# Latent attention whose keys and queries come transposed out of their products, with one product for all rotary parts and another order of the first layer's loads and splits

## Chip, core and metric

The kernel runs on one core of a Trainium2 chip. The metric is the device time of one execution in microseconds. The core has TensorE for matrix products (PE; PEld is its load of the stationary operand), VectorE (DVE), ScalarE (ACT), GpSimd (POOL), and SyncE (SP), which here only issues the transfers. Products land in PSUM, eight banks of 128 partitions by 512 words; everything else is held in SBUF with 128 partitions.

## What is computed

A decoder of four layers on 256 tokens of width 1024. Layers 0 and 3 mix tokens by multi-head latent attention, layer 1 by a convolution, layer 2 by a gated recurrence; every layer then has a SwiGLU feed-forward and an embedding that is gated by the residual stream. The change touches the attention of layers 0 and 3 and the start of layer 0. Cut to that:

```python
def _mla(u, positions, w_in, q_norm_g, w_uq, kv_norm_g, w_ukv, w_out):
    c = u @ w_in                                  # 1024 -> 384 + 256 + 32
    c_q, c_kv, k_r = jnp.split(c, [384, 640], axis=-1)
    q = (_rmsnorm(c_q, q_norm_g) @ w_uq).reshape(B, S, 16, 64 + 32)
    kv = (_rmsnorm(c_kv, kv_norm_g) @ w_ukv).reshape(B, S, 16, 64 + 64)
    q_nope, q_rope = jnp.split(q, [64], axis=-1)
    k_nope, v = jnp.split(kv, [64], axis=-1)
    q_rope, k_rope = _rope(q_rope, cos, sin), _rope(k_r, cos, sin)
    q = concat([q_nope, q_rope]); k = concat([k_nope, k_rope for every head])
    o = _causal_attention(q, k, v, 96 ** -0.5)    # 16 heads, softmax over earlier tokens
    return o.reshape(B, S, 1024) @ w_out
```

## The kernel before

All large products are made in three partial products of rounded halves. An operand x is split into hi (x rounded to the matrix format) and lo (the rest): for activations in `split`, hi on ACT (L237) and lo on DVE (L238), for weights in `granule`, hi on ACT (L180, or L185 with a gain folded in) and lo on DVE (L181, L186). `mm` then issues hi·hi, hi·lo and lo·hi (all L207). Weights come in granules of 128 rows by 1024 words by one transfer each (L176 on SP) into four `raw` buffers, are split into nine `whi` and eight `wlo` buffers, and are used once. A later granule's load thus waits until a raw buffer has been split, and its split until an earlier granule has been used. `self.fence` names an instruction on ACT and one on DVE behind which the next splits are put into the queues; `issue_after` does that for a block.

The program is written as one sequence; a list scheduler interleaves it into the queues of the engines by program order and readiness, and each engine then runs its queue in order.

**The start (`run`).** The gains and the first 128 tokens are loaded, `mla_setup` loads the positions, makes the causal mask and computes the rotation angles in some thirty small DVE operations, then the first input weight is loaded and split, `Norm.do(0)` takes squares of the tokens on ACT (L73) and transposes them on TensorE (L250) into the split operand xT, then the same for the other 128 tokens, then the other seven input weights.

**The head of an attention layer (`mla`).** For each of two halves of 128 tokens the input projection lands in two PSUM banks, is copied (`cg`), squared for the second norm, transposed and split into the operand cT (640 rows by 256 tokens). In layer 0 `rope_tables` takes the sine (L535). A chain of small DVE operations (`rsqrt`) makes the scales `sc` of the second norm, and the rotary key `krot` is rotated.

**The heads.** `heads(gi)` makes the queries, keys and values of four heads. For each half of the tokens it multiplies cT (stationary) with the query weights (4 x 96 = 384 columns) and with the key and value weights (512 columns). Tokens lie on partitions, so that ACT applies the scale per token when it evicts the queries (L619) and the values (L625), and DVE that of the keys (L622). POOL copies the rotated key into each head (L623), DVE rotates the queries' last 32 columns (L549 to L552), and TensorE transposes each head's queries and keys, 128 x 96 to 96 x 128 (L631), eight transposes for each half of the tokens, which ACT (L635) and DVE (L637) evict into qT and kT.

**Attention.** `attend(gi)` takes a group in two steps of two heads: scores of both token blocks into two banks (L645 to L650), maxima on DVE (L652 to L654), exponentials with row sums on ACT (L659), scaling by the reciprocal on DVE and ACT (L666, L668), transposes (L672 to L678), evictions (L675, L679) and the weighted sums (L682, L684). `heads(gi)` is issued before `attend(gi - 1)`.

**The end of the layer.** Behind the last group's heads, the output weights (eight granules) are loaded and split, in layer 0 after the layer's embedding weights (`embed_weights`), and the embedding's 24 products (`embed`) are issued after the last `attend`. The first six k-tiles of the output projection of the first tokens can run before the last group is done (`linear`, with `early`).

## Time and profile before

| | us |
|---|---|
| median of 3 runs | 1402.48 |
| lowest and highest of them | 1398.79, 1409.24 |
| the profiled execution | 1401.64 |
| its span, from first to last instruction | 1399.9 |
| layer 0: input projection done, first scores, last weighted sum, feed-forward | 31.2, 50.5, 116.6, 135.6 |
| layer 3: the same | 1082, 1102.4, 1164.4, 1175.4 |
| granted TensorE clock, mean | 0.993 |

The times of the stages are read from the timeline. A group's row gives the source line, engine and operation, what it writes and reads, the shapes, the count, and behind the bar the busy time and the mean ns of one, then the idle time of the engine before it and what ended that. A row of the timeline gives start, duration, and the same names. A matmul's duration there runs until its last result has landed, and so overlaps the next one's.

### The profile page before, as it was taken

To read this page: it belongs to the slowest core of one execution; us is meant where nothing else is said; L and a number is where in the kernel's file an instruction comes from. 1 tells how busy PE (TensorE), PEld (TensorE's weight loads), DVE (VectorE), ACT (ScalarE), POOL (GpSimd) and SP (SyncE) were. 2 spreads that over 40 slices of the span, in tenths; PEclk is the share of its full clock that TensorE was granted. 3 is DMA by queue.
4 is the path that set the end of the run, shared out by engine and by line. 5 is a ranking of instruction groups with operands and counts; after the bars stand their busy time and mean duration, and the time that the engine had idled before them with its cause. 6 is when DMAs were issued, how large, how long until landed. Compare 5 with 4: busy or idle time off the path is not lost.

```text
span 1399.9 us, 20414 instructions
## 1 busy us (share of the span) xinstructions
PE 1340.7 (96%) x7153; PEld 1094.1 (78%) x7153; DVE 920.0 (66%) x1995; ACT 789.0 (56%) x1493; POOL 15.6 (1%) x51
## 2 busy tenths in 40 slices
PE   7889999999898999999999999999999999999997
PEld 6757878887886788888788887878878767788885
DVE  6774555548786855556887768555567776555556
ACT  6684545546625754455675546555556776554543
POOL 0000000000000000000000000000000000000000
PEclk9999999999999999999999999999999999999998
DMA  7242655555674666554474435655553433666632
GB/s 217 94 140 87 210 181 181 181 180 167 187 226 153 187 196 190 181 181 142 132 223 125 140 91 166 195 181 181 181 171 111 136 121 108 207 192 190 187 126 76
DMA packets 174023, 228.15 MB, mean 163 GB/s; under 512 B 11712, under 2 KB 138848, under 8 KB 173920
## 3 DMA queue, kind: packets, MB, share of 16 engines
q1 hardware_dynamic: 173920, 226.85, 52.1%
q8 instruction: 56, 0.92, 0.3%
q14 instruction: 47, 0.39, 0.1%
HBM read 222.27 MB, written 1.05 MB: 160 GB/s over the span
## 4 chain that ended last, share of the span: by engine, by line
PE 76%; DVE 8%; DMA 7%; ACT 6%; issue 3%; SPq 0%; DVEq 0%; ACTq 0%
PE mm L207 41%; PE acc L207 26%; PE tr L250 3%; DVE wlo L186 3%; DMA raw<-in_ffn_w_down_dram 2%; DMA raw<-in_ple_w_gate_dram 1%; PE acc L1013 1%; ACT whi L180 1%; ACT whi L185 1%; DMA raw<-in_mla_w_out_dram 1%; ACT p L659 1%; DVE wlo L181 1%; PE acc L649 1%; DMA raw<-in_ffn_w_gu_dram 1%; DMA raw<-in_conv_w_pw_dram 1%
## 5 line engine op out<-in xcount | busy, mean ns | idle before, releaser
L207 PE MATMUL mm<-whi,xT 128*128 128x512 f32 x1632 | 546.8, 398 | 1.2 <-ACT xT L237 0.9
L185 ACT ACTIVATE whi<-raw,gT 128x512 fp32r<-128x512 f32 (+3 forms) x604 | 387.0, 701 | 133.4 <-PE acc L207 59.7
L186 DVE SCALAR_TENSOR_TENSOR wlo<-raw,gT,whi 128x512 fp32r<-128x512 f32 (+3 forms) x604 | 410.1, 728 | 52.0 <-PE acc L207 33.1
L207 PEld LDWEIGHTS mm<-whi,xT 128*128 128x128 f32 x1632 | 305.6, 188 | 63.5 <-ACT xT L237 1.4
L207 PE MATMUL mm<-wlo,xT 128*128 128x512 f32 x816 | 320.6, 393 | 1.1 <-DVE wlo L181 1.1
L207 PE MATMUL acc<-whi,aT 128*128 128x512 f32 x704 | 233.1, 392 | 1.7 <-DVE aT L238 1.7
L181 DVE TENSOR_TENSOR wlo<-raw,whi 128x1024 fp32r<-128x1024 f32 x120 | 146.7, 1224 | 75.3 <-ACT whi L180 75.0
L180 ACT ACTIVATE whi<-raw 128x1024 fp32r<-128x1024 f32 x120 | 126.0, 1059 | 95.3 <-DMA raw<-in_ffn_w_down_dram 58.2
L207 PEld LDWEIGHTS mm<-wlo,xT 128*128 128x128 f32 x816 | 153.6, 188 | 30.6 <-DVE wlo L181 1.4
L207 PE MATMUL acc<-whi,xT 128*128 128x512 f32 (+2 forms) x544 | 167.1, 382 | 6.2 <-ACT xT L237 6.2
L207 PEld LDWEIGHTS acc<-whi,aT 128*128 128x128 f32 x704 | 131.5, 188 | 35.3 <-DVE aT L238 4.1
L207 PE MATMUL acc<-wlo,aT 128*128 128x512 f32 x352 | 138.7, 394 | 0.0
L364 DVE SCALAR_TENSOR_TENSOR ga<-mm,rs_y,sg 128x256 f32<-128x256 f32 x88 | 42.4, 481 | 139.9 <-ACT sg L362 139.9
L207 PEld LDWEIGHTS acc<-whi,xT 128*128 128x128 f32 x544 | 100.5, 190 | 22.4 <-ACT xT L237 7.0
L362 ACT ACTIVATE sg<-mm,rs_y 128x256 f32<-128x256 f32 x88 | 41.0, 466 | 134.8 <-PE mm L207 134.7
L207 PE MATMUL acc<-wlo,xT 128*128 128x512 f32 (+2 forms) x272 | 101.9, 375 | 0.0
L207 PEld LDWEIGHTS acc<-wlo,aT 128*128 128x128 f32 x352 | 66.2, 188 | 13.0
L238 DVE TENSOR_TENSOR aT<-tr,aT 128x256 fp32r<-128x256 f32 x88 | 37.0, 421 | 55.3 <-ACT aT L237 55.3
L207 PEld LDWEIGHTS acc<-wlo,xT 128*128 128x128 f32 x272 | 51.7, 190 | 7.6
L207 PE MATMUL mm<-whi,cT 128*128 128x384 f32 (+1 forms) x160 | 51.4, 381 | 5.7 <-ACT q L619 4.7
L73 ACT ACTIVATE junk<-h 128x512 bf16<-128x512 f32 x48 | 30.0, 625 | 45.8 <-DVE h L339 25.0
L237 ACT ACTIVATE aT<-tr 128x256 fp32r<-128x256 f32 x88 | 32.7, 371 | 28.1 <-PE tr L250 28.0
(250 smaller groups left out, 1455.4 us busy)
## 6 DMA issues: line engine op xcount, KB each, us to landing
raw<-in_ffn_w_gu_dram SPq DMA_DIRECT2D x352, 256.0 KB, 4.4
raw<-in_ffn_w_down_dram SPq DMA_DIRECT2D x88, 512.0 KB, 4.3
raw<-in_ple_w_gate_dram SPq DMA_DIRECT2D x32, 512.0 KB, 4.7
raw<-in_hgrn_w_in_dram SPq DMA_DIRECT2D x64, 256.0 KB, 3.8
raw<-in_mla_w_out_dram SPq DMA_DIRECT2D x16, 512.0 KB, 4.4
raw<-in_conv_w_pw_dram SPq DMA_DIRECT2D x32, 256.0 KB, 4.8
raw<-in_mla_w_in_dram SPq DMA_DIRECT2D x16, 336.0 KB, 3.8
raw<-in_mla_w_uq_dram SPq DMA_DIRECT2D x12, 384.0 KB, 3.8
```

Of the source, the lines that this page charges most:

```text
L73: square = nc.scalar.activation(T.tmp("junk", [P, 512], 1, BF16), h[:, s], AF.Square, accum_out=ss[:, c : c + 1])
L180: nc.scalar.activation(hi[:, :used], raw[:, :used], AF.Copy)
L181: nc.vector.tensor_tensor(out=lo[:, :used], in0=raw[:, :used], in1=hi[:, :used].bitcast(F32), op=ALU.subtract)
L185: nc.scalar.activation(hi[:, s], raw[:, s], AF.Copy, scale=g[k])
L186: nc.vector.scalar_tensor_tensor(out=lo[:, s], in0=raw[:, s], scalar=g[k], in1=hi[:, s].bitcast(F32), op0=ALU.mult, op1=ALU.subtract)
L207: ins = self.nc.tensor.matmul(*args, **kw)
L237: a = self.nc.scalar.activation(hi, src, AF.Copy)
L238: v = self.nc.vector.tensor_tensor(out=lo, in0=src, in1=hi.bitcast(F32), op=ALU.subtract)
L250: nc.tensor.transpose(pt[:, (i - k0) * P : (i - k0 + 1) * P], src[:, i * P : (i + 1) * P], self.ident)
L362: nc.scalar.activation(sg, ps[:, :256], AF.Silu, scale=r)
L364: nc.vector.scalar_tensor_tensor(out=ga, in0=ps[:, 256:], scalar=r, in1=sg, op0=ALU.mult, op1=ALU.mult)
L649: nc.tensor.matmul(s1[:, hh], qT[:HD, h, P:], kT[:HD, h], start=True, stop=False)
```

## The change

**Products.** The weights are laid out anew on the host: all heads' plain query columns, then all rotary query columns; all keys, then all values. Queries and keys are now made with the weights as the stationary operand and cT, all 256 tokens wide, as the moving one, so that they come out with head channels on partitions and tokens along the columns. One product holds two heads (2 x 64 channels); `queries` evicts the lower 64 partitions on ACT and the upper 64 on DVE, `keys` both on DVE. The scale of a key is no longer one per partition: it is spread over columns by a product of ones with a diagonal matrix (`kscale`) and multiplied in at the eviction. The queries stay unscaled; their scale goes into the softmax, per token (`scl`, `nscl`). Values are made for eight heads at once.

**Rotary parts.** The rotary query columns of all 16 heads come out of one product per half of the tokens, are rotated at once (`rope` with 512 columns) and transposed four heads at a time (`rotary`). The rotated key is repeated four times, transposed, and copied by POOL into its 32 rows of each head's keys. A head's 96 channels lie among 128 rows, and the rows that belong to other heads are zero in the keys (`memset`), so the scores contract over 128 rows.

**The first layer.** The tokens are loaded first, then the gains, then the weights; the tokens' transposes come before the squares of the norm, which are put behind the last split of the input weights; the masks and the angles come after all input weights; the embedding's weights are loaded and split before attention, and its products run right after the input projection.

```diff
-            for t in range(NT):
-                ss, r = css[t], norm.r[t]
...
             if i == 0:
+                self.embed(0)
                 self.rope_tables()
...
+            ws = weights(0)
+            wr = self.ktiles(wq, [(D, 512)], gq)
+            self.fence = split
 
             qTs, kTs = (self.tmp("xT", [P, 2, HG, S], 4) for _ in range(2))
+            for rows, h in ((96, 0), (64, 1), (0, 2), (32, 3)):
+                nc.gpsimd.memset(kTs[rows : rows + 32, :, h], 0.0)
...
+            def pairs(gi, w, xs):
+
+                ps = self.bank("mm", 2)
+                c = (gi % 2) * 256
+                for m in range(2):
+                    s = slice(c + m * P, c + (m + 1) * P)
+                    self.mms(ps[:, m * S : (m + 1) * S], [(hi[:, s], lo[:, s]) for hi, lo in w], xs)
+                return ps.rearrange("p (m n) -> p m n", m=2)
+
+            def queries(gi, w):
+                ps = pairs(gi, w[0], cTT[:3])
+                q = qTs[:, gi % 2]
+                nc.scalar.activation(q[LOW, 0:2], ps[LOW], AF.Copy)
+                V.tensor_copy(q[HIGH, 2:4], ps[HIGH])
+
+            def keys(gi, w):
+                ps = pairs(gi, w[1], cTT[3:])
+                k = kTs[:, gi % 2]
+                for rows, hs in ((LOW, slice(0, 2)), (HIGH, slice(2, 4))):
+                    last = V.tensor_tensor(out=k[rows, hs], in0=ps[rows], in1=kscale[rows, None, :].to_broadcast([64, 2, S]), op=ALU.mult)
+                return last
...
+            def rotary(gi):
+
+                q = qTs[:, gi % 2]
+                pt = self.bank("tr", 2)[:, :S]
+                for t in range(NT):
+                    nc.tensor.transpose(pt[:, t * P : (t + 1) * P], qr[t].rearrange("p h d -> p (h d)")[:, gi * P : (gi + 1) * P], self.ident)
+                for h in range(2):
+                    nc.scalar.activation(q[HIGH, h], pt[HIGH], AF.Copy)
+                for h in range(2):
+                    V.tensor_copy(q[LOW, 2 + h], pt[LOW])
+
+            queries(0, ws)
...
+                dg = tmp("diag", [P, P], 2)
+                V.tensor_scalar(out=dg, in0=self.ident, scalar1=s[:, 1:2], scalar2=None, op0=ALU.mult)
+                nc.tensor.matmul(pk[:, t * P : (t + 1) * P], self.ones, dg, start=True, stop=True)
...
+            for rows, h in ((64, 0), (96, 1), (32, 2), (0, 3)):
+                for b in range(2):
+                    nc.gpsimd.tensor_copy(kTs[rows : rows + 32, b, h], krT[rows : rows + 32])
+            qr = []
+            for t in range(NT):
+                ps = self.bank("mm", 2)
+                self.mms(ps, self.cut(cT, t, 0, 3), wr)
+                q = tmp("qr", [P, NH, ROPE], 2)
+                self.rope(q, ps.rearrange("p (h d) -> p h d", d=ROPE), t, pool)
+                qr.append(q)
+            keys(0, ws)
+            vs = values(ws)
+            rotary(0)
...
+            for gi in range(1, NH // HG):
+                if gi == 1:
+                    ws1 = weights(1)
+                w = ws if gi < 2 else ws1
+                queries(gi, w)
+                rotary(gi)
+                keys(gi, w)
+                before = vs
+                if gi == 2:
+                    vs = values(w)
+                last = attend(gi - 1, before, self.acc)
+                if gi == 2:
+                    self.fence = last
+            wo = self.halves(a["mla_w_out"][j])
+            attend(NH // HG - 1, vs, self.acc)
...
         load(0)
+        self.nc.sync.dma_start(self.gT, a["gains"])
+        self.head = self.mla_head(0, range(2))
+        n1.transposed(0)
+        load(1)
+        self.head += self.mla_head(0, range(2, 4))
+        self.fence = n1.transposed(1)
+        self.head += self.mla_head(0, range(4, KD))
+        self.masks()
+        with self.tc.issue_after(self.last_split.ins):
+            for t in range(NT):
+                n1.stats(t, operand=False)
         self.mla_setup()
-        self.head = self.mla_head(0, range(1))
-        n1.do(0)
-        load(1)
-        self.head += self.mla_head(0, range(1, 2))
-        n1.do(1)
-        self.head += self.mla_head(0, range(2, KD))
+        self.embed_weights(0)
```

173 lines of the change are left out of this document (85 added, 88 removed).

## Prediction

> **What bounds the kernel now.** I read the page first (busy shares, chain), then the windows by stage, the waits of TensorE, and last the timeline and the groups for the price of single instructions.
>
> ```profile
> PE 1340.7 (96%) x7153; PEld 1094.1 (78%) x7153; DVE 920.0 (66%) x1995; ACT 789.0 (56%) x1493; POOL 15.6 (1%) x51
> ...
> PE 76%; DVE 8%; DMA 7%; ACT 6%; issue 3%; SPq 0%; DVEq 0%; ACTq 0%
> ```
>
> TensorE bounds the whole: 96% busy, 76% of the chain. The change touches only the start and the two attention layers (0 and 3), so their stages decide. In the windows below the columns are stretch, length, busy time and count of PE, PEld, DVE, ACT, POOL, then granted clock and DMA.
>
> ```profile
> 31.20:50.50 19.30, 17.03 (x92) 15.15 (x90) 17.41 (x58) 13.33 (x26) 2.36 (x3) 0.91 0.51 150
> 50.50:116.60 66.10, 57.06 (x343) 42.13 (x341) 41.55 (x100) 46.25 (x122) 1.24 (x4) 0.95 0.32 103
> 116.60:135.60 19.00, 19.00 (x92) 15.58 (x90) 10.54 (x26) 8.64 (x17) 0.00 (x0) 1.00 0.30 88
> ...
> 1082.00:1102.40 20.40, 19.34 (x119) 16.91 (x118) 18.74 (x55) 16.03 (x31) 2.46 (x4) 1.00 0.54 182
> 1102.40:1164.40 62.00, 56.88 (x350) 42.11 (x349) 38.85 (x97) 42.38 (x115) 1.02 (x3) 1.00 0.28 87
> 1164.40:1175.40 11.00, 11.00 (x56) 8.98 (x55) 8.00 (x21) 7.94 (x16) 0.00 (x0) 1.00 0.10 21
> ```
>
> For each of the two layers these are the head (from the end of the input projection to the first scores), the attention stage, and the rest of the output projection. In the heads DVE is as much the bound as TensorE (17.4 of 19.3 us, 18.7 of 20.4). In the attention stages TensorE is busiest, and ACT and DVE have room (42.4 and 38.9 of 62). From the first scores to the feed-forward, layer 0 takes 66.1 + 19.0 = 85.1 us and layer 3 takes 62.0 + 11.0 = 73.0.
>
> ```profile
> PE acc L207 <- ACT xT L237: 5.2, 1, 5.2
> PE tr L672 <- DVE p L666: 4.1, 2, 3.9
> PE mm L207 <- ACT q L619: 3.8, 2, 2.3
> ```
>
> These are TensorE's long waits up to 120 us (total, times, longest): at the start, late in layer 0's attention, and for the eviction of a query product.
>
> **The products.** A matmul's duration overlaps the next one's, so I price by the spacing of starts in a steady run.
>
> ```profile
> 1165.58 2.73 PE mm L207 x12
> ...
> 43.22 0.51 PE L207 MATMUL mm<-whi,cT 128*128 128x384 f32 x2
> 43.57 0.34 PE L207 MATMUL mm<-wlo,cT 128*128 128x384 f32 x1
> ...
> 366.60 0.40 PE L207 MATMUL acc<-xT,whi 128*128 128x256 f32 x2
> 366.84 0.28 PE L207 MATMUL acc<-xT,wlo 128*128 128x256 f32 x1
> ...
> 46.49 0.87 PE tr L631 x8
> ```
>
> 512 columns cost 2.73/12 = 0.227 us, 384 cost (43.57 - 43.22)/2 = 0.173, 256 cost (366.84 - 366.60)/2 = 0.120, a transpose 0.87/8 = 0.109. Before, a layer runs 72 products of 384 columns (4 groups, 2 token halves, 3 k-tiles, 3 partial products), 48 of 512, and 64 transposes: 12.5 + 10.9 + 7.0 = 30.4 us. After, it runs 120 products of 256 (72 for queries, 48 for keys), 42 of 512 (24 for values, 18 for all rotary parts), and 12 small ones (8 query and 2 key transposes, 2 diagonal products, taken at a transpose's price): 14.4 + 9.5 + 1.3 = 25.2. That is 5.2 us less TensorE work per layer, nearly all of it in the attention stage: the head did 15.2 of the old 30.4, and will do 14.4 of the new (first two groups' queries and keys, one half of the values, all rotary parts).
>
> The scores now contract over 128 rows, not 96. Rows of both heights with 128 columns agree, so I take nothing:
>
> ```profile
> L648 PE MATMUL acc<-xT,xT 96*128 96x128 f32 x64 | 12.6, 289 | 0.0
> ...
> L995 PE MATMUL acc<-q,kb 128*128 128x128 f32 x32 | 5.3, 287 | 1.4 <-ACT kb L983 1.4
> ```
>
> **ACT and DVE.** Groups by form, with mean ns of one behind the comma:
>
> ```profile
> L186 DVE SCALAR_TENSOR_TENSOR wlo<-raw,gT,whi 128x512 fp32r<-128x512 f32 x512 | 356.5, 746 | 44.0 <-PE acc L207 32.6 <-ACT whi L185 10.5 <-issue 0.7
> ...
> L637 DVE COPY xT<-tr 96x512 f32<-96x512 f32 x16 | 10.9, 681 | 2.3 <-PE tr L631 2.3
> ...
> L635 ACT ACTIVATE xT<-tr 96x512 f32<-96x512 f32 x16 | 9.5, 593 | 4.4 <-PE tr L631 4.3
> ...
> L619 ACT ACTIVATE q<-mm,csc 128x384 f32<-128x384 f32 x16 | 9.3, 583 | 8.9 <-PE mm L207 8.7
> L622 DVE TENSOR_SCALAR k<-mm,csc 128x256 f32<-128x256 f32 x16 | 7.7, 479 | 4.3 <-PE mm L207 4.3
> ...
> L625 ACT ACTIVATE v<-mm,csc 128x256 f32<-128x256 f32 x16 | 7.6, 475 | 3.5 <-DVE k L622 3.3
> ```
>
> ACT loses per layer 8 x (0.583 + 0.475 + 0.593) = 13.2 us; it gains 4 query and 4 value evictions at 0.593 and 9 rotary ones of 256 columns at 0.475 at most: 9.0. DVE loses 8 x (0.479 + 0.681) = 9.3 and 32 small rotations; it gains 4 query and 8 key evictions at 0.681, 9 of 256 columns at 0.479 and two wide rotations of four operations (two at 0.48, two at 0.68): 8.2 + 4.3 + 4.6 = 17.1. The small rotations were 32 operations of 64 or 128 columns, each under the 0.479 of 256, so DVE ends between 7.8 worse and, were they 0.479 each, 7.5 better; I take even. The same weight columns are split in three more pieces, under 3 x 0.75. So ACT gets lighter and DVE does not: the heads, DVE's own stages, don't shrink. Of the 5.2 us I keep 4 per layer (ends: 0 if the chain of ACT and DVE sets the pace of attention, 5.2 if TensorE does). What speaks for most of it is that the chain can run faster than it does:
>
> ```profile
> 1149.32 0.33 PE tr L672
> ...
> 1154.46 0.22 PE tr L672 x2
> ```
>
> Two steps of attention (two heads each) start their transposes 5.1 us apart here; 8 steps at that pace are 41 of the 62 us.
>
> **A new wait.** The diagonal products that spread the key scale over columns wait for DVE's chain of small operations on the second norm, and the key transposes for the rotation. Behind them on TensorE stand the rotary, key and value products, and all scores wait for those. In layer 0 the embedding's products stand in front as cover (5.4 us). In layer 3 there are none, but its head of 20.4 us held 15.2 us of products and will hold 14.4, so 6.0 us of such waits fit before it grows; I cost it at nothing, and at 1 us for each us beyond that.
>
> **The start.** Below are the timeline's rows for the first weights, first product, positions, last input weights and the sine.
>
> ```profile
> 1.65 0.43 SPq L477 DMA_DIRECT2D pos_i<-in_positions_dram  x1
> ...
> 8.80 0.85 ACT L185 ACTIVATE whi<-raw,gT 128x672 fp32r<-128x672 f32 x1 [3.00 <-DMA raw<-in_mla_w_in_dram]
> ...
> 12.31 0.69 PE L207 MATMUL acc<-whi,xT 128*128 128x384 f32 x1 [5.18 <-ACT xT L237]
> ...
> 15.08 4.50 SPq L176 DMA_DIRECT2D raw<-in_mla_w_in_dram  x3
> ...
> 19.88 0.26 ACT L535 ACTIVATE angle<-angle 128x64 f32<-128x64 f32 x1
> ```
>
> The squares of the norm stood on ACT ahead of the transposes' eviction; now they come last, and the first product can start when the first weights are split: 8.80 + 0.85 = 9.65, that is 2.7 us earlier. Against it: the positions' load falls behind eight weight loads on SP's queue, from 1.65 to 19.6 at the latest, and the sine then from 19.88 to 38 at the latest; the rotated keys must be ready by the first scores at 50, so 12 us are left for their rotation and copies. The queries' eviction no longer needs the norm's scale, so the 2.3 us wait on L619 should go. But DVE, dense through this head, now also splits the embedding's two weight tiles there, and the embedding's 24 products (5.4 us) fill TensorE. I take 1 us gained up to the first scores (ends: 6.7 gained, which is 2.7 + 2.3 + 1.7 for the slow clock below; 5 lost, if the sine's lateness shows).
>
> ```profile
> 35.00:37.30 2.30, 0.07 (x1) 0.00 (x0) 2.16 (x17) 2.30 (x5) 0.30 (x1) 1.00 0.55 165
> 37.30:40.70 3.40, 3.35 (x14) 3.16 (x15) 2.73 (x12) 1.63 (x3) 0.00 (x0) 0.56 0.00 0
> ```
>
> A stall of 2.3 us was followed by 3.4 us at 0.56 of the clock, so it cost about 1.7 us more than itself. The Trainium skill, "TensorE: Matmul & The Clock Gate", Part 1, lets the clock fall after an idle window of about 3.4 us. By that rule a 2.3 us stall would cost itself alone, and the upper end would be 5.0; the trace has it shorter.
>
> **Layer 0's late attention.** There the embedding's splits stood in front of the output weights', and TensorE's 3.9 us wait lies behind this piece of the chain:
>
> ```profile
> 93.37 5.05 DMA raw<-in_mla_w_out_dram
> ```
>
> With the embedding gone, layer 0 runs the same queue as layer 3, which has none of it: 85.1 - 73.0 = 12.1 us (5.4 of products, the rest stall and slow clock). I take 12. If the stall stays, 5.4; it cannot be under 0 unless the cover is missed, which is the third rival.
>
> **The sum.** 4 + 4 + 1 + 12 = 21 us off the profiled execution's 1401.64 us (span 1399.9) gives 1380.6, say 1381; the median shown, 1402.48, is 0.8 us above that execution. The other stages keep their code.
>
> **Rivals.** *All of it lands:* 5.2 + 5.2 + 6.7 + 12.1 = 29, 1372. For it: the waits named above all lie on what is removed. Against: DVE's dense heads.
>
> *Attention keeps its pace:* ACT and DVE set it, and the 5.2 us turn into idle TensorE; in the place of the removed products nothing covers the chain. With nothing from the start and 5.4 from the embedding alone it gives 1396. For it: both stages already show idle TensorE (66.1 - 57.1 = 9.0 and 5.1 us).
>
> *Key copies:* the rotated keys go by eight copies on POOL, seven of them before the first scores.
>
> ```profile
> 36.22 0.30 POOL L623 COPY k<-kr 128x128 f32<-128x128 f32 x1 [5.35 <-DVE kr L552]
> 41.19 1.69 POOL L623 COPY k<-kr 128x128 f32<-128x128 f32 x1 [4.68 <-PE tr L631]
> ```
>
> The same copy took 0.30 and, beside DVE's splits, 1.69 us. I count 0.6 each for twice the columns, 4.2 in all, covered by the rotary, key, value and next query and key products behind them (4.1 + 1.4 + 2.7 + 2.2 + 1.4 = 11.8 us). At 2 x 1.69 they take 23.7, 11.9 uncovered and 1.7 of slow clock, in two layers 27: 1408. The Trainium skill, "GPSIMD Engine Reference", section 8, says that GpSimd shares its SBUF interfaces with VectorE and contends with DVE instructions that have two SBUF inputs, as L186's have. The trace agrees, by the 1.69.
>
> *Slower:* with half the products gone between attention steps, the output weights' splits stand on ACT ahead of the exponentials and wait for their loads, as once in layer 0 (3.9 + 1.7 = 5.6 us each time). Eight of the 16 weight tiles can arrive late (four fit the raw buffers): 8 x 5.6 = 45 gives 1426. It decides, past 1% slower, from (21 + 14)/5.6 = 6.3 places on; against it, layer 3 shows none that long.
>
> **The numbers.** Forecast (1374 to 1388) 0.45; all of it (under 1374) 0.20; attention keeps its pace or slow copies (1388 to 1416) 0.27; slower 0.08. One per cent, 14 us, is about what a measurement can tell from no change. Faster by over 1% (below 1388): 0.45 + 0.20 = 0.65; within 1%: 0.27; slower: 0.08. The range runs from 1366, some 6 us past everything landing, to 1396, where attention keeps its pace; the forecast's own is 1374 to 1388.
>
> **What would show it.** Right: 120 products of 256 columns a layer near 0.120 us apart; no wait of TensorE on a query eviction; layer 0 and layer 3 within 3 us from first scores to feed-forward, both near 69; first product near 9.7 us; the sine before 38. Wrong: attention stages still about 62 us with more idle TensorE; POOL copies over 1.7 us with the first scores waiting on POOL; a wait of over 3 us of the softmax transposes on DVE in either layer.

## The result and the profile after

| | before | after |
|---|---|---|
| median, us | 1402.32 | 1417.66 |
| lowest to highest | 1398.79 to 1409.24 | 1415.75 to 1421.36 |
| ratio, 95% interval | | 1.0102 [1.0065, 1.0139] |
| profiled execution, span | 1401.64, 1399.9 | 1421.36, 1419.6 |
| granted clock, mean | 0.993 | 0.978 |

The changed kernel is slower by 1.0%. The forecast was 1381 us with a range from 1366 to 1396. In the new program all line numbers have moved: products are L216, splits of weights with a gain L194 and L195, exponentials L727, transposes of the softmax L740 to L746.

The page of the changed kernel, busy time by engine and the chain of work that ended last:

```profile
PE 1350.9 (95%) x7137; PEld 1097.6 (77%) x7137; DVE 925.9 (65%) x1975; ACT 789.2 (56%) x1485; POOL 24.1 (2%) x63
...
PE 75%; DVE 11%; DMA 6%; ACT 5%; issue 3%; SPq 0%; DVEq 0%; ACTq 0%
```

TensorE's busy time rose by 10 us, though the change takes product work away; that already points to the clock. DVE's share of the chain went from 8% to 11%.

The windows of the changed kernel, for head (end of the input projection to first scores) and attention stage (first scores to last weighted sum) of layer 0 and of layer 3; columns as in the prediction:

```profile
29.80:56.50 26.70, 23.98 (x132) 18.55 (x132) 26.27 (x81) 19.14 (x41) 6.48 (x10) 1.00 0.61 196
56.50:130.80 74.30, 62.16 (x332) 44.66 (x330) 37.72 (x82) 42.60 (x108) 0.00 (x0) 0.84 0.20 65
1094.90:1117.70 22.80, 18.48 (x107) 15.66 (x106) 20.81 (x55) 12.91 (x26) 5.22 (x9) 0.93 0.60 192
1117.70:1185.60 67.90, 56.77 (x332) 40.67 (x330) 36.42 (x80) 42.49 (x108) 0.00 (x0) 0.92 0.21 67
```

The kernel before, cut at the same events, and below it timeline rows of layer 3: its first scores, those of the second head of the same pair, its first maxima, and the first maxima of the changed kernel:

```profile
31.30:50.50 19.20, 16.93 (x91) 15.05 (x90) 17.31 (x58) 13.23 (x26) 2.36 (x3) 0.91 0.51 150
50.50:116.70 66.20, 57.16 (x344) 42.23 (x342) 41.55 (x100) 46.25 (x122) 1.24 (x4) 0.95 0.32 102
1084.90:1098.30 13.40, 13.14 (x78) 11.60 (x77) 13.19 (x45) 9.47 (x19) 1.98 (x3) 1.00 0.51 169
1098.30:1164.50 66.20, 60.28 (x369) 44.63 (x368) 42.14 (x104) 46.04 (x121) 1.49 (x4) 1.00 0.31 102
```

```profile
1098.25 0.39 PE L648 MATMUL acc<-xT,xT 96*128 96x128 f32 x2
1102.31 0.44 PE L648 MATMUL acc<-xT,xT 96*128 96x128 f32 x2
1103.11 0.42 DVE L652 TENSOR_REDUCE mx<-acc 128x2 f32<-128x256 f32 x1
...
1119.35 0.42 DVE L720 TENSOR_REDUCE mx<-acc 128x2 f32<-128x256 f32 x1
```

The prediction had put layer 3's first scores at 1102.4 us and the end of the input projection at 1082; those of the timeline are 1098.25 and 1084.9. (1102.4 is the second head of the first pair.) By the first scores, layer 3 grew by 9.4 us in the head and 1.7 in the attention stage. In the head TensorE is busy 5.3 us longer and idle 4.1 us longer (22.80 - 18.48 = 4.3, before 0.3). In the attention stage it is busy 3.5 us less but idle 5.2 us more (11.1, before 5.9), and its clock fell from 1.00 to 0.92.

This cut is kind to the kernel before. It runs six more products of 512 columns and eight transposes between the scores of its first two heads, and the softmax can't begin before both are there, since the maxima are taken over the pair. Cut at the first maxima instead, layer 3 of the kernel before and then of the changed one:

```profile
1084.90:1103.10 18.20, 17.14 (x102) 14.57 (x100) 17.16 (x54) 13.47 (x27) 2.46 (x4) 1.00 0.60 203
1103.10:1164.50 61.40, 56.28 (x346) 41.66 (x345) 38.17 (x95) 42.04 (x114) 1.02 (x3) 1.00 0.27 86
1094.90:1119.30 24.40, 20.08 (x118) 16.97 (x117) 22.36 (x57) 12.91 (x26) 5.22 (x9) 0.93 0.60 192
1119.30:1185.60 66.30, 55.17 (x322) 39.36 (x320) 34.88 (x78) 42.49 (x108) 0.00 (x0) 0.92 0.21 64
```

By this cut the head grew by 6.2 us (2.9 busy, 3.3 idle) and the rest by 4.9. The sum is the same; 3.2 us of the head's 9.4 come from where the cut falls. Below, windows start at the first scores unless the maxima are named. Layer 0 grew by 7.5 us in the head, where the embedding's 5.4 us now stand, and by 8.1 in the attention stage, whose clock is 0.84; from there to the feed-forward it got 7.9 us back (18.9 to 11.0).

What the windows don't say is why TensorE's 5 us less of product work turned into idle time. The waits of TensorE up to 140 us (total, times, longest):

```profile
PE tr L740 <- DVE p L734: 5.0, 4, 2.8
PE tr L259 <- POOL xT L623: 4.7, 1, 4.7
PE acc L216 <- ACT xT L246: 4.4, 1, 4.4
PE acc L717 <- ACT p L727: 3.3, 2, 2.3
```

In attention it waits for the scaled probabilities (L740 on L734) and for a score bank that the exponentials still read (L717 on L727): the chain of one softmax step, from scores over maxima, exponentials, reciprocal and scaling to transposes. Windows around these waits show what follows them:

```profile
60.50:63.90 3.40, 1.19 (x11) 0.98 (x9) 0.00 (x0) 3.36 (x9) 0.00 (x0) 1.00 0.00 0
63.90:70.70 6.80, 5.77 (x24) 4.13 (x25) 2.12 (x6) 2.10 (x4) 0.00 (x0) 0.50 0.00 0
91.20:98.00 6.80, 6.17 (x22) 4.01 (x22) 3.98 (x11) 5.62 (x16) 0.00 (x0) 0.50 0.24 77
...
111.70:121.90 10.20, 9.03 (x31) 6.29 (x30) 3.35 (x8) 5.08 (x14) 0.00 (x0) 0.50 0.25 81
1122.00:1125.40 3.40, 1.75 (x15) 1.37 (x13) 0.66 (x3) 2.93 (x10) 0.00 (x0) 1.00 0.00 0
1125.40:1128.80 3.40, 2.93 (x15) 1.78 (x15) 0.42 (x1) 0.60 (x1) 0.00 (x0) 0.50 0.00 0
```

A stretch of 3.4 us in which TensorE was busy for 1.19 or 1.75 us only is followed by 3.4 or 6.8 us at half clock. Layer 0's attention has 6.8 + 6.8 + 10.2 = 23.8 us at half clock.

### The profile page after: what moved, and what is told of

Read it like the earlier page. It is cut to its first block, busy times and chain, and to the rows that moved or that the text cites. A ratio compares the mean times of both kernels' runs of the same rounds, so it can differ in the third digit from the quotient of the medians.

```text
span 1419.6 us, 20340 instructions
## 1 busy us (share of the span) xinstructions
PE 1350.9 (95%) x7137; PEld 1097.6 (77%) x7137; DVE 925.9 (65%) x1975; ACT 789.2 (56%) x1485; POOL 24.1 (2%) x63
## 4 chain that ended last, share of the span: by engine, by line
PE 75%; DVE 11%; DMA 6%; ACT 5%; issue 3%; SPq 0%; DVEq 0%; ACTq 0%
PE mm L216 40%; PE acc L216 26%; DVE wlo L195 3%; PE tr L259 3%; DMA raw<-in_ple_w_gate_dram 1%; ACT p L727 1%; PE acc L1081 1%; DMA raw<-in_conv_w_pw_dram 1%; PE acc L717 1%; ACT whi L194 1%; DMA raw<-in_ffn_w_down_dram 1%; DVE wlo L190 1%; DMA raw<-in_mla_w_out_dram 1%; ACT xT L246 1%; DVE xT L247 1%
## 5 line engine op out<-in xcount | busy, mean ns | idle before, releaser
L216 PE MATMUL mm<-whi,xT 128*128 128x512 f32 x1632 | 551.5, 401 | 1.7 <-ACT xT L246 1.7
L194 ACT ACTIVATE whi<-raw,gT 128x512 fp32r<-128x512 f32 (+2 forms) x610 | 388.7, 697 | 130.8 <-PE acc L216 60.5
L195 DVE SCALAR_TENSOR_TENSOR wlo<-raw,gT,whi 128x512 fp32r<-128x512 f32 (+2 forms) x610 | 410.7, 723 | 55.2 <-PE acc L216 32.6
L216 PEld LDWEIGHTS mm<-whi,xT 128*128 128x128 f32 x1632 | 308.1, 190 | 64.8 <-ACT xT L246 2.6
L216 PE MATMUL mm<-wlo,xT 128*128 128x512 f32 x816 | 323.4, 396 | 0.9 <-DVE wlo L190 0.7
L216 PE MATMUL acc<-whi,aT 128*128 128x512 f32 x704 | 233.1, 392 | 2.2 <-DVE aT L247 2.2
L216 PEld LDWEIGHTS mm<-wlo,xT 128*128 128x128 f32 x816 | 154.9, 190 | 32.6 <-DVE wlo L190 2.9
L216 PE MATMUL acc<-whi,xT 128*128 128x512 f32 (+2 forms) x544 | 166.8, 382 | 5.3 <-ACT xT L246 5.3
L216 PEld LDWEIGHTS acc<-whi,aT 128*128 128x128 f32 x704 | 131.6, 188 | 35.6 <-DVE aT L247 4.5
L216 PE MATMUL acc<-wlo,aT 128*128 128x512 f32 x352 | 138.6, 394 | 0.0
L216 PEld LDWEIGHTS acc<-whi,xT 128*128 128x128 f32 x544 | 100.5, 190 | 21.5 <-ACT xT L246 6.2
L216 PE MATMUL acc<-wlo,xT 128*128 128x512 f32 (+2 forms) x272 | 102.2, 377 | 0.0
L216 PEld LDWEIGHTS acc<-wlo,aT 128*128 128x128 f32 x352 | 66.2, 188 | 13.0
L216 PEld LDWEIGHTS acc<-wlo,xT 128*128 128x128 f32 x272 | 51.7, 190 | 7.5
L216 PE MATMUL acc<-xT,whi 128*128 128x256 f32 x256 | 48.2, 290 | 0.6 <-DVE xT L247 0.3
L216 PE MATMUL mm<-xT,whi 128*128 128x256 f32 x256 | 47.9, 285 | 0.0
```

Of the source, the lines that this page charges most:

```text
L194: self.last_split = nc.scalar.activation(hi[:, s], raw[:, s], AF.Copy, scale=g[k])
L195: nc.vector.scalar_tensor_tensor(out=lo[:, s], in0=raw[:, s], scalar=g[k], in1=hi[:, s].bitcast(F32), op0=ALU.mult, op1=ALU.subtract)
L216: ins = self.nc.tensor.matmul(*args, **kw)
```

## Experiments

All kernels were timed against the kernel before, on the same chip as their neighbours in a group; its median there was 1401.29 to 1402.72 us. Differences between kernels below go by the medians, and by the ratios where they matter; one of 2 or 3 us between two groups is within the intervals.

| kernel | median, us | ratio to before, 95% interval |
|---|---|---|
| changed kernel | 1417.66 | 1.0102 [1.0065, 1.0139] |
| products only | 1423.58 | 1.0145 [1.0123, 1.0168] |
| start only | 1395.24 | 0.9949 [0.9931, 0.9967] |
| one scale | 1411.34 | 1.0066 [1.0041, 1.0092] |
| useless products | 1409.18 | 1.0045 [1.0029, 1.0061] |
| start only + useless products | 1400.54 | 0.9993 [0.9979, 1.0006] |
| one scale + useless products | 1406.16 | 1.0030 [1.0011, 1.0050] |
| late weights | 1416.47 | 1.0115 [1.0095, 1.0134] |
| late weights, late rotary | 1419.63 | 1.0136 [1.0114, 1.0158] |
| the same + useless products | 1413.22 | 1.0085 [1.0064, 1.0105] |
| a third of the products | 1415.21 | 1.0088 [1.0068, 1.0108] |
| the same + useless products | 1409.47 | 1.0047 [1.0028, 1.0066] |
| attention first | 1430.18 | 1.0206 [1.0180, 1.0232] |
| the same + useless products | 1430.06 | 1.0196 [1.0167, 1.0225] |
| start only, attention first | 1423.02 | 1.0154 [1.0130, 1.0177] |
| no division | 1399.07 | 0.9978 [0.9963, 0.9994] |
| start only, no division | 1395.69 | 0.9956 [0.9941, 0.9970] |
| fenced weights | 1424.56 | 1.0167 [1.0148, 1.0185] |
| no wide rotation | 1412.40 | 1.0080 [1.0064, 1.0096] |

### The two halves of the change

Products only keeps the old start and the embedding's old place; start only keeps the old products. The edits, against the changed kernel (the second also takes `mla`, `rope` and `ktiles` from the kernel before):

```diff
 products only
             if i == 0:
-                self.embed(0)
                 self.rope_tables()
...
+            if i == 0:
+                self.embed_weights(0)
             wo = self.halves(a["mla_w_out"][j])
             attend(NH // HG - 1, vs, self.acc)
+            if i == 0:
+                self.embed(0)
...
-        self.head = self.mla_head(0, range(2))
-        n1.transposed(0)
...
+        self.head = self.mla_head(0, range(1))
+        n1.do(0)
```

```diff
 start only
-            ws = weights(0)
-            wr = self.ktiles(wq, [(D, 512)], gq)
...
+            for t in range(NT):
+                ss, r = css[t], norm.r[t]
...
+            def heads(gi):
```

> The transposed products and the rotary product alone, with the start and the embedding's place as before. Theory A (the attention stages got longer because the chain of maxima, exponentials and copies now has less TensorE work beside it, longer exponentials, and a slower TensorE clock): still slower than before, layer 3 by about 10 us as in the changed kernel, layer 0 by less because the embedding's products are cover again; 1407 to 1418 us. Theory B (the start and the moved embedding cost the time): faster than before by the 10.4 us of removed products, about 1390 us.

> The new start and the embedding's new place alone, with the products as before. Theory A: the input projection ends 1 to 2 us earlier, layer 3 keeps its 144 us between feed-forwards, and the time is 1395 to 1402 us. Theory B: slower than before, about 1415 us, the whole of it in layer 0.

The halves add within their intervals: against the kernel before in the same group (1402.72 us) the products cost 20.9 us, more than theory A had (1423.58 us, against 1407 to 1418), and the new start gains 7.5. So the start paid, and the whole loss is in the products. The windows of start only, layer 0 and layer 3:

```profile
29.80:53.70 23.90, 21.70 (x116) 18.11 (x116) 22.68 (x77) 19.59 (x38) 2.69 (x5) 1.00 0.68 220
53.70:117.00 63.30, 57.68 (x355) 42.78 (x353) 38.30 (x96) 42.13 (x114) 0.96 (x4) 1.00 0.23 76
```

```profile
1081.40:1094.70 13.30, 13.04 (x76) 11.50 (x75) 13.09 (x45) 9.42 (x19) 1.98 (x3) 1.00 0.55 176
1094.70:1160.50 65.80, 60.25 (x369) 44.60 (x368) 42.21 (x104) 45.98 (x121) 1.49 (x4) 1.00 0.31 101
```

Layer 3 stands where it stood before. In layer 0 the head grew by 4.7 us (the embedding's products, 5.4), the input projection ended 1.5 earlier, the attention stage lost 2.9 and the tail to the feed-forward 7.9.

### The scale in the exponentials

The changed kernel gives each exponential a scale per token (`scl`), where the kernel before had a constant:

```diff
-    V.tensor_tensor(out=mx, in0=mx, in1=nscl[:, :, None].to_broadcast([P, 2, 2]), op=ALU.mult)
+    V.tensor_scalar(out=mx, in0=mx, scalar1=-scale, scalar2=None, op0=ALU.mult)
...
-    p[:, hh], s[:, hh], AF.Exp, scale=scl[:, t : t + 1], bias=mx[:, t, hh : hh + 1],
+    p[:, hh], s[:, hh], AF.Exp, scale=scale, bias=mx[:, t, hh : hh + 1],
```

> The changed kernel, but the softmax takes one constant scale as before, and so leaves out the norm of the queries. It asks what the per-token scale of the exponentials costs. Theory A: the exponentials return from 0.45 and 0.56 us to about 0.36 and 0.48, which is 0.35 us on the chain of each of 16 steps, 5.6 us in all: about 1412 us. If attention is not bound by its chain: within 1 us of the changed kernel's 1417.7.

The groups of the exponentials, in the kernel before, the changed kernel, and with one scale:

```profile
L659 ACT ACTIVATE p<-acc,mx 128x256 f32<-128x256 f32 x32 | 14.9, 479 | 0.0
L659 ACT ACTIVATE p<-acc,mx 128x128 f32<-128x128 f32 x32 | 11.4, 364 | 17.2 <-DVE mx L654 17.2
```

```profile
L727 ACT ACTIVATE p<-acc,mx,scl 128x256 f32<-128x256 f32 x32 | 17.7, 562 | 0.0
L727 ACT ACTIVATE p<-acc,mx,scl 128x128 f32<-128x128 f32 x32 | 14.4, 452 | 19.2 <-DVE mx L722 18.9
```

```profile
L727 ACT ACTIVATE p<-acc,mx 128x256 f32<-128x256 f32 x32 | 14.8, 475 | 0.0
L727 ACT ACTIVATE p<-acc,mx 128x128 f32<-128x128 f32 x32 | 11.4, 362 | 18.6 <-DVE mx L722 18.5
```

The scale as an operand costs 0.083 us (256 columns, 562 - 479) or 0.088 us (128 columns, 452 - 364) for each of the 64 exponentials, 5.5 us in all. The Trainium skill, "ScalarE: Activation LUTs", section "What ACT_TABLE_LOAD costs", says that each operand of one value per partition adds about 93 ns; the trace agrees, with 83 and 88 ns against the kernel before. The time fell by 6.3 us, as expected; the two kernels' intervals overlap in part, so the rows carry the size and the time only agrees with it. How it reached the time is not told apart here: in the profiled execution the clock of the two attention stages rose as well, from 0.84 and 0.92 to 0.92 and 0.97.

### The clock

Ten products whose result nobody reads are put behind the scores of each of the 16 softmax steps, which adds work to TensorE and nothing else:

```diff
+                    self.idle(10)
                     mx = tmp("mx", [P, 2, 2], 3)
```

> The changed kernel with ten products of 128 x 256 (about 1.1 us at full clock) that nothing reads, behind the scores of each of the 16 attention steps: 17.6 us more TensorE work. If the slow clock is the larger part of the loss, the granted clock in the attention stages returns to 1.00 and the time falls to 1403 to 1412 us. If the chain alone sets the pace and the slow clock only accompanies it: 1415 to 1420 us. If TensorE is the bound: about 1435 us.

> The kernel with the new start and the old products (1395.2 us, no half-clock stretch in either attention layer), with the same ten useless products behind the scores of each of the 16 softmax steps. Clock theory: there is no slow clock to mend, so they cost a part of their 17.6 us: 1400 to 1412 us. If they helped the changed kernel by another way than the clock (by the order of TensorE's queue), they help here too: 1395 us or less.

> The changed kernel with constant scales in the exponentials and the maxima (the queries' norm is left out, as in the kernel with one scale) and the ten useless products behind the scores. One scale alone was worth 6.3 us, the useless products alone 8.5. If the slower exponentials and the slow clock are two costs: 1401 to 1405 us. If the slower exponentials cost by way of the clock (they make the gaps in which it falls): no better than the better of the two, 1407 to 1411 us.

The windows of the changed kernel with useless products: layer 0's attention stage, then head and attention stage of layer 3:

```profile
55.80:121.50 65.70, 60.55 (x412) 45.86 (x410) 37.65 (x82) 42.36 (x108) 0.00 (x0) 1.00 0.23 73
1085.20:1109.10 23.90, 19.89 (x107) 16.58 (x106) 20.74 (x54) 12.85 (x26) 5.23 (x9) 0.86 0.60 197
1109.10:1174.10 65.00, 60.43 (x412) 45.92 (x410) 36.46 (x80) 42.38 (x108) 0.00 (x0) 1.00 0.21 66
```

With 17.6 us more work for TensorE the kernel is 8.5 us faster: both attention stages run at a clock of 1.00, and layer 0's falls from 74.3 to 65.7 us. In the kernel with the old products, where the clock was 1.00 without them, the same products cost 5.3 us. So the slow clock costs the changed kernel some 8.5 us, or more if the useless products are not free here either, and the thinning out of the products in attention brought it. With one scale too, the time falls between the two forecasts, and the gains don't add fully: 11.5 us together, 6.3 and 8.5 alone. Behind the useless products one scale is worth 3.0 us. Part of what the slower exponentials cost thus went by way of the gaps in which the clock falls, or is now hidden by the useless products themselves; these runs don't separate the two.

### What paces the attention stage

First the product work itself. Of the three partial products of the plain queries, keys and values, one is kept (shown for queries and keys, the values are cut alike):

```diff
-  self.mms(ps[:, m * S : (m + 1) * S], [(hi[:, s], lo[:, s]) for hi, lo in w], xs)
+  for k, (x, y) in enumerate(zip(w, xs)):
+      self.matmul(ps[:, m * S : (m + 1) * S], x[0][:, s], y[0], start=k == 0, stop=k == len(xs) - 1)
```

> The changed kernel with one of three partial products (hi times hi) of the plain queries, the keys and the values; the other two are left out, so these operands are less exact. That is 48 + 32 products of 256 columns and 16 of 512 less in each attention layer, 13.2 us of TensorE by the spacings, half of it ahead of the first scores and half behind them. If TensorE's work sets the pace: 6 to 7 us off the attention stage (67.9 us in the second attention layer) and as much off the head, 1391 to 1395 us in all. If the serial chain of a softmax step on ACT and DVE sets it: the attention stage stays at 65 to 70 us with some 17 us of idle TensorE, perhaps at a still slower clock, and the kernel stands at 1405 to 1418 us.

> The same with a third of the partial products, and ten useless products behind the scores of each softmax step to hold the clock. To compare with the changed kernel with the useless products alone (1409.2 us, attention stage of the second attention layer 65.1 us). Chain theory: the attention stage stays within 2 us of 65.1 at a granted clock of 1.00, the head is 3 to 6 us shorter, the kernel 1398 to 1406 us. TensorE theory: the attention stage falls by 6.6 us to about 58.5 and the kernel to about 1383 us.

Windows of layer 3, head and attention stage, with a third of the products, and then with useless products added:

```profile
1088.30:1106.60 18.30, 11.92 (x49) 7.64 (x48) 17.09 (x48) 11.33 (x23) 5.21 (x9) 0.88 0.62 200
1106.60:1180.00 73.40, 56.48 (x293) 38.99 (x291) 39.90 (x87) 43.99 (x111) 0.00 (x0) 0.85 0.23 72
```

```profile
1087.20:1105.40 18.20, 11.86 (x48) 7.58 (x47) 17.02 (x47) 11.08 (x23) 5.22 (x9) 0.84 0.60 200
1105.40:1174.60 69.20, 59.52 (x373) 43.10 (x371) 39.60 (x87) 43.80 (x111) 0.00 (x0) 0.94 0.23 77
```

Some 26 us of TensorE work were taken out of the kernel, and the time fell by 2.5 us, and by nothing where the useless products stood (there 1398 to 1406 us had been forecast for a chain that sets the pace). By the first scores the head got shorter by 4.5 to 5.7 us and the attention stage longer, from 67.9 to 73.4 us and from 65.0 to 69.2. But here the scores of the second head come 4.1 us behind those of the first. By the first maxima neither moved: the head took 24.4 us before and after (25.5 and 24.3 with the useless products), though it holds 6.6 us less work, with 10.2 us at half clock in it now; the rest took 66.2 and 67.3 us (63.5 and 63.1). So in the attention stage product work does not set the pace any more; what the head would have gained at full clock, these runs don't show.

Then the chain of a step itself, in the changed kernel and in the one with the old products:

```diff
-                    rc = tmp("rc", [P, NT, 2], 3)
-                    recip = V.reciprocal(rc, sums)
-                    for hh in range(2):
-                        V.tensor_scalar(out=p0[:, hh], in0=p0[:, hh], scalar1=rc[:, 0, hh : hh + 1], scalar2=None, op0=ALU.mult)
-                    for hh in range(2):
-                        copy = nc.scalar.activation(p1[:, hh], p1[:, hh], AF.Copy, scale=rc[:, 1, hh : hh + 1])
```

> The changed kernel without the division of the softmax: the reciprocal, the two scalings on VectorE and the two on ScalarE of every softmax step are left out, so that the transposes wait for the exponentials alone. In the rows that takes about 1.2 us out of each step's serial chain (0.18 reciprocal, 0.25 wait, 0.9 scaling), no TensorE work at all. Chain theory: 12 to 19 us off in 16 steps, 1399 to 1406 us. If TensorE's work (or its order alone) sets the pace: within 4 us of 1417.7; at a still slower clock, perhaps.

> The same part left out of the kernel with the new start and the old products (1395.2 us), where TensorE was busy 60.3 of 66.2 us in the second attention layer. If the old products leave TensorE as the bound of the attention stage: under 6 us off, 1389 to 1396 us. If the old kernel's steps were paced by the same chain: 12 to 19 us off, 1376 to 1383 us.

Layer 3's windows, of the changed kernel without the division, then of the old products without it:

```profile
1081.00:1105.00 24.00, 19.92 (x107) 16.64 (x105) 20.80 (x54) 12.78 (x26) 5.23 (x9) 0.86 0.59 195
1105.00:1163.50 58.50, 50.74 (x329) 37.60 (x328) 30.78 (x56) 35.50 (x92) 0.00 (x0) 1.00 0.23 73
```

```profile
1077.30:1090.60 13.30, 13.04 (x77) 11.50 (x76) 13.09 (x45) 9.46 (x19) 1.98 (x3) 1.00 0.55 170
1090.60:1154.90 64.30, 60.15 (x361) 43.36 (x359) 37.47 (x80) 39.23 (x105) 1.50 (x4) 0.97 0.32 104
```

This is the pair that settles it. The same part left out, with no TensorE work in it, is worth 18.6 us with the new products and nothing with the old ones (1395.69 against 1395.24). Part of the 18.6 is the clock, which is back at 1.00 in this stage. Against the useless products, at the same clock, the kernel is 10.1 us faster, and the stage fell from 65.0 to 58.5 us, 0.8 us for each of 8 steps. The edit also makes ACT and DVE lighter, but in the changed kernel neither was near full (42.5 and 36.4 of 67.9 us). The old products left TensorE as the main bound of the attention stage; not quite the only one, since in the profiled executions the stages of the kernel without the division are 3.1 us (layer 0) and 1.5 us (layer 3, at a clock of 0.97) shorter, which the medians don't show. The new products made TensorE so light that the softmax chain is the bound.

### The head

The first theory for the longer head was VectorE's order: the small operations of the second norm, on which the keys wait, run between splits of 0.75 us of weights that are needed much later, and between the wide rotations. Late weights moves those splits in program order, late rotary moves the rotary product and its rotations behind keys and values, and the third adds the useless products:

```diff
             for gi in range(1, NH // HG):
-                if gi == 1:
-                    ws1 = weights(1)
...
                 last = attend(gi - 1, before, self.acc)
+                if gi == 1:
+                    ws1 = weights(1)
```

> The changed kernel with one edit: the weights of heads 8 to 15 are loaded and split behind the first attention instead of ahead of it. In the changed kernel their splits (seven of 0.75 us on VectorE) stand between the small instructions of the second norm, from whose result the keys wait (norm ready at 1109.2 us, first scores 22.8 us behind the end of the first projection in the second attention layer). Theory A (the head is longer because the norm's chain shares VectorE with these splits and the wide rotations): the head falls by about 3 to 4 us in each of the two layers, to about 19 us; the kernel to 1409 to 1413 us. Theory B (the head is longer only because TensorE work moved into it, 5.3 us by the busy time): the head stays within 1 us of 22.8 and the time within 3 us of 1417.7.

> As the kernel with late weights, and the rotary product of all heads with its four wide rotations a token tile (2.2 us of VectorE each tile) issued behind the keys and values. Theory A (VectorE's order in the head): the norm's chain has VectorE to itself and the keys are evicted some 5 us earlier, the head about 17 to 19 us, the kernel 1405 to 1411 us. Theory B (TensorE work alone): within 3 us of 1417.7; the rotary eviction, now late, takes the keys' place as the last wait.

> As the kernel with late weights and late rotary product, and with ten useless products behind the scores of each of the 16 softmax steps (17.6 us of TensorE at full clock). If the two causes, the slow clock in attention (worth 8.5 us when the same products were put into the changed kernel) and VectorE's order in the head, are separate, their gains add: 1396 to 1403 us. If the useless products only fill the time that VectorE's order leaves, they cost what they last here: at or over the time of the kernel without them.

Late weights was a blunt test: the scheduler still ran twelve splits of VectorE in the head, as many as in the changed kernel, and the head lasted 23.7 us. With the rotary product late too, the norm was ready 11.9 us behind the input projection (14.3 in the changed kernel) and the keys were evicted 3.4 us sooner, but the head got no shorter. With the useless products as well the time is 1413.22 us: they gain 6.4 us here, with the attention stage at 64.8 us and a clock of 1.00, and the 1396 to 1403 of the forecast, which needed a shorter head, did not come. The window of the head with both late:

```profile
1089.00:1113.40 24.40, 19.81 (x110) 15.86 (x108) 21.38 (x52) 12.09 (x25) 3.71 (x9) 0.93 0.58 192
```

So these two orders are not it. The second theory was that group 1's queries and keys stand in front of the first scores. Attention is issued first, in the changed kernel, with useless products, and in the kernel with the old products (there ahead of `heads`):

```diff
+                last = attend(gi - 1, vs, self.acc)
                 queries(gi, w)
                 rotary(gi)
                 keys(gi, w)
-                before = vs
                 if gi == 2:
                     vs = values(w)
-                last = attend(gi - 1, before, self.acc)
```

> The changed kernel with each attention instruction block issued ahead of the next group's queries, rotary parts and keys instead of behind them (program order sets the scheduler's preference). In the changed kernel the queries and keys of group 1 (30 products, 3.6 us) run ahead of the first scores. Theory A (the head is longer because group 1's products stand in front of the first scores, and the steps of attention, paced by their serial chain, cannot give the time back): the head of the second attention layer falls from 22.8 to 19 or 20 us, the attention stage stays within 2 us of 67.9, the kernel 1410 to 1414 us. Theory B (the products are only placed where TensorE waits anyway, for the rotary parts on VectorE): the head falls by under 1.5 us and what it gains is lost in the attention stage: within 3 us of 1417.7, or slower, since less product work is left ready to run beside a step.

> The changed kernel with attention first and the ten useless products behind the scores of each softmax step. To compare with the useless products alone (1409.2 us; head 23.9, attention stage 65.0 us in the second attention layer). Theory A: head 20 to 21 us, attention stage 64 to 66, kernel 1402 to 1406 us. Theory B: within 3 us of 1409.2, or slower.

> The same edit in the kernel with the new start and the old products (1395.2 us): attention issued ahead of the next group's heads. If the steps' serial chain paces attention there too, earlier scores shorten the layer: 1386 to 1393 us. If TensorE's work paces it, as the 60.3 us of busy time in 66.2 suggest, the time stays within 3 us of 1395.2 or rises.

Layer 3 of the changed kernel with attention first, head and attention stage:

```profile
1096.50:1116.30 19.80, 14.88 (x76) 12.10 (x75) 18.64 (x51) 10.94 (x22) 5.07 (x9) 0.91 0.61 203
1116.30:1195.80 79.50, 62.26 (x364) 45.92 (x362) 39.48 (x84) 44.77 (x112) 0.00 (x0) 0.91 0.19 62
```

The head falls by 3 us as theory A has it, and the attention stage grows by 11.6; theory B had only the sign of that ("or slower"), and its head of under 1.5 us less did not come. With the useless products the time is the same, 1430.06 us, where theory A had 1402 to 1406; here they don't bring the clock back to 1.00 (0.96 and 0.93 in the two attention stages). In the kernel with the old products the edit costs 27.8 us. The next group's products in front of a group's attention are no ballast. Without them there TensorE idles 17.2 us in the stage, 11.1 with them; that the next group's evictions, rotations and transposes then lie bare between two groups is likely, but no run shows it by itself.

The last two runs take VectorE's work itself out of the head, the splits by a fence behind the first attention, and the wide rotations by a plain copy:

```diff
 fenced weights, beside late weights
+                if gi == 1:
+                    self.fence = last
+                    ws1 = weights(1)
```

```diff
 no wide rotation
-                self.rope(q, ps.rearrange("p (h d) -> p h d", d=ROPE), t, pool)
+                V.tensor_copy(q.rearrange("p h d -> p (h d)"), ps)
```

> As the kernel with late weights, but the splits of the weights of heads 8 to 15 are now held behind the first attention's reciprocal and scaling, so that they do leave the head (in the kernel with late weights the scheduler still ran twelve splits of VectorE there, as many as in the changed kernel). VectorE is busy 20.8 of 22.8 us in the head of the second attention layer, and in every variant so far the head lasts one to three us more than VectorE's busy time in it. Theory A (VectorE's amount of work bounds the head): about 4 us of splits leave, the head falls to 18.5 to 20 us. Theory B (the products ahead of the first scores bound it): the head stays at 22 to 24. What it gains may be lost where the later queries wait for the late splits, so the head is the measure, not the time (1408 to 1425 us).

> The changed kernel with one copy in place of the four operations of each wide rotation of the queries (the rotation of the queries is left out): about 3 us less VectorE work in each head, no TensorE work, no other place touched. Theory A (VectorE bounds the head): the head of the second attention layer falls by 2.5 to 3.5 us to about 19.5 to 20.3, the kernel by 4 to 7 us to 1411 to 1414. Theory B (products bound it): head within 1 us of 22.8 to 23.9, kernel within 3 us of 1417.7.

Layer 3's heads in the two:

```profile
1090.60:1111.10 20.50, 17.14 (x107) 13.96 (x106) 16.33 (x47) 8.47 (x19) 3.31 (x9) 1.00 0.39 126
```

```profile
1090.70:1112.80 22.10, 18.85 (x106) 15.60 (x105) 18.99 (x48) 12.73 (x26) 5.02 (x9) 0.92 0.66 211
```

Neither theory holds whole. VectorE lost 4.5 us of work in the first and 1.8 in the second, the head 2.3 and 0.7; in the first, 1.3 of the 2.3 is TensorE's same 107 products at a clock of 1.00. The whole kernel got slower with the fence, 1424.56 us, as the attention stage of layer 3 grew from 67.9 to 71.1 us. Without the wide rotation it took 1412.40 us, as theory A forecast, but not by the head: layer 0's attention stage fell from 74.3 to 69.3 us, its clock rose from 0.84 to 0.90.

With the clock at 1.00 the first row lets the head's 9.4 us be told apart by TensorE's time: 17.14 - 13.14 = 4.0 us is more work ahead of the first scores, 18.48 - 17.14 = 1.3 us is the slow clock, 4.1 us is idle time. Up to the first scores the head held 36 products of 384 columns, 18 of 512 and 16 transposes before (12.1 us at the prediction's prices), and 60 of 256, 30 of 512 and 10 small ones after (15.1 us). Up to the first maxima it held 24 of 512 and 24 transposes before, 14.3 us in all, so by that cut there is little more work: the 6.2 us are 1.6 of work (18.74 us busy at a clock of 1.00 with the fence, 17.14 before), 1.3 of slow clock and 3.3 of idle time. TensorE's longest wait in this idle time is 2.1 us for the rotated queries (L216 on qr of L568, DVE). It is 0.2 us with the fence and gone without the wide rotation, where waits for an eviction of the values (L654) grow from 0.5 to 1.1 us. So for each microsecond taken from VectorE in the last run the head yields about 0.4 us. What else holds it, with VectorE busy 20.8 of 22.8 us and a chain of evictions behind it, stays open.

## Why the prediction was wrong

**The products.** The work did fall about as counted (the two diagonal products a layer are four short ones, 0.2 us more). The products of 256 columns start 0.115 us apart (predicted 0.120):

```profile
1114.31 0.40 PE L216 MATMUL mm<-cT,whi 128*128 128x256 f32 x2
1114.54 0.28 PE L216 MATMUL mm<-cT,wlo 128*128 128x256 f32 x1
```

The step that failed is "Of the 5.2 us I keep 4 per layer". Its ground was that the chain of ACT and DVE "can run faster than it does", from two steps 5.1 us apart. Those were two steps of one group that overlap; a whole group of the kernel before took about 14 us, TensorE was busy in nearly all of it, and there was little to take before the chain became the pace. In place of 4 us gained, layer 3 lost 11.1 from the end of its input projection to its last weighted sum (79.5 to 90.6 us). The placement was off too: the prediction had 0.8 us less product work in the head and 4.4 less behind it. By the counts up to the first maxima it is 0.8 us more in the head and 5.7 us less behind it (36, 24 and 40 of the old kinds, 60, 12 and 4 of the new), where it was worth nothing. The rival "attention keeps its pace" was the right one in kind, and too mild: it kept the pace, and put no price on the slow clock or the exponentials.

**The exponentials' scale** was not priced at all: 5.5 us by the rows. The prediction listed ACT's evictions and passed over the operand that 64 exponentials gained. ACT was to lose 4.2 us a layer; its busy time stayed (789.0 and 789.2).

**The clock** was priced only as what follows a stall (1.7 us each time). In the changed kernel it is a cost of some 8.5 us, and it comes with the forecast itself: work taken from TensorE in a stage with a chain beside it makes the thin stretches in which the clock falls.

**A new wait** "at nothing": up to the first maxima TensorE idles 3.3 us more in layer 3's head, and a half-clock stretch adds 1.3. The bound on it ("6.0 us of such waits fit before it grows") took for idle all of the old head that the counted products did not fill. But the prediction's own window has TensorE busy 19.34 of these 20.40 us; up to the first maxima it was 17.14 of 18.20. There was room for about 1 us.

**The start** came out 1.3 us earlier, not 2.7: the first product starts at 10.98. It waits for ACT's eviction of the tokens' transposes (L246 at 10.35), and that stands behind three splits of weights (L194, from 7.67 to 10.44), where the prediction put one. Ahead of these splits ACT loads its function table for 1.28 us, from 6.37 on, when the first weights have landed; in the kernel before it did so at 0.73, before there was anything to wait for. The clearing of the keys on POOL, to which the row of L259 above puts a wait of 4.7 us, is not the cause: start only has no clearing, its transposes begin at 4.72 us (4.69 here), and its first product at 10.89. The sine was on time, with ten us in hand. The timeline:

```profile
10.98 0.69 PE L216 MATMUL acc<-whi,xT 128*128 128x384 f32 x1 [4.35 <-ACT xT L246]
...
27.69 0.26 ACT L552 ACTIVATE angle<-angle 128x64 f32<-128x64 f32 x1
```

The first scores were to come 1 us earlier; start only shows them 3.2 us later (50.5 to 53.7), because the embedding's 5.4 us of products did not fill waits there. **Layer 0's late attention** was to give 12 us, from a difference of 85.1 and 73.0. With layer 3's first scores at 1098.25 the second number is 77.2 and the difference 7.9; from the first maxima on (51.87 and 1103.11) it would be 83.7 - 72.3 = 11.4. Start only measures 10.8 (from first scores to feed-forward, 85.1 to 74.3). So the mechanism was right and the 12 near, though by two cuts that do not match; the 1 us that the start was to gain came out as 3.2 lost. Together they gave 7.6 us in the profile, 7.5 in the medians, where 13 were forecast.

**The other rivals.** The key copies took what was counted:

```profile
L695 POOL COPY xT<-krT 32x256 f32<-32x256 f32 x16 | 9.6, 625 | 9.6 <-ACT krT L692 9.4
```

0.625 us against 0.6. From first scores to feed-forward the changed kernel takes 85.3 us in layer 0 and 78.8 in layer 3, where the prediction wanted both near 69. The slower case was forecast by late loads of the output weights; the one wait of over 3 us that would have shown it did not come (the longest of the softmax transposes on DVE is 2.8 us). The kernel ended slower by another mechanism than the one that stood for it.

**The version that beats both** is start only, 1395.24 us, 0.9949 [0.9931, 0.9967] of the kernel before.

## What to carry to other kernels

Work taken from the busiest engine of a stage is worth only what lies between that engine and the chain beside it: leave out a piece of the chain before and after, and see which of the two kernels it moves. Count the operands that an edit adds to instructions on the chain, not only the instructions that it adds or removes. And cut stages at rows of the timeline, at the instruction that starts the chain and not only at the first of a name: the same layer grew by 9.4 and 1.7 us by one cut, and by 6.2 and 4.9 by the other.

## What the runs showed of the hardware

TensorE's clock fell without a full stall. Stretches of 3.4 us in which TensorE was busy 35% (1.19 of 3.40) or 51% (1.75 of 3.40) were followed by half clock, for 3.4, 6.8 or 10.2 us, multiples of one length. The Trainium skill, "TensorE: Matmul & The Clock Gate", Part 1, has the clock fall after an idle window of about 3.4 us; the length agrees with the trace, but the window need not be idle. As a consequence a kernel got faster, from 1.0102 to 1.0045 of the time before, by 160 products whose results are thrown away.
